# A delta-rule stage whose planner keeps a begun run of fill matmuls for three, with three more planning weights changed

## The chip, the cores and the metric

The kernel runs on one core of one Trainium2 chip. The metric is the device time of one execution in microseconds. Engines are called as in the profile: PE is TensorE (matmuls), PEld its weight loads, DVE is VectorE, ACT ScalarE, POOL GpSimd, and SP the engine that issues the DMAs. A line such as L886 is line 886 of the kernel before; from line 93 on, the same statement of the changed kernel stands 2 to 5 lines lower.

## What is computed

One layer of a diffusion backbone on 1024 latent tokens with a prefix of 256 context tokens, width 1024, 8 heads in each of two branches. Branch A is a gated delta rule, scanned forwards and backwards over chunks; branch B is differential softmax attention. Both are gated, projected, merged and projected once more. Cut to what matters here:

```python
h  = rms_norm(x)   * (1 + scale)   + shift      # 1024 latent tokens
hc = rms_norm(ctx) * (1 + scale_c) + shift_c    # 256 context tokens
qkv_a, z_a, a, b, q_b, k_b, v_b, z_b, gates = split_cols(h @ w_in)   # the context likewise

# branch A, for each direction and head, over chunks, one after the other
def step(s, xs_i):
    u_i, w_i, kd_i, gl_i, qd_i, qk_i = xs_i
    v_new  = u_i - w_i @ s
    s_next = s * exp(gl_i) + kd_i.T @ v_new
    return s_next, qd_i @ s + qk_i @ v_new

# branch B, for each head and block of queries
p = softmax(q @ k.T * scale)                    # two maps to a head
o = (p[0] - lam * p[1]) @ v

y_a = rms_norm(o_a) * silu(z_a);  y_b = rms_norm(o_b) * (1 - lambda_init) * silu(z_b)
merged = sigmoid(g_a) * (y_a @ w_oa) + sigmoid(g_b) * (y_b @ w_ob)
x = x + gate * (merged @ w_out)
```

## The kernel before

Everything is on one core, in float32 accuracy: a big matmul is made of three matmuls on a high and a low part of each operand (`wh`, `wl` of the weights, two tiles `hs` of the tokens). The program goes through five stages:

- **Front and first projections** (to about 420 us): tokens are normed and transposed, and the columns for branch A's q, k and v are projected, convolved and stored.
- **Delta-rule stage** (about 420 to 1300 us), the function `flow`, which the change edits. Here run side by side: the preparation of each head (`gdn_prep`: tiles `gram`, `pz`, `p2`, `p3`, `pu6` on PE), two scans, one for each direction (`scan`, L1292 on), the output of each chunk (`out_chunk`), the tails of finished heads (`tails`, tiles `oT`), and **fill**: projections that nothing in this stage needs soon. Fill is first attention's q, k and v columns (`part_flow`, 256-column matmuls) and then 32 units of gate columns (`fill_flow`, 512-column matmuls `mm<-hs,wh` and `mm<-hs,wl`; a unit is two times 24 of them).
- **Hand-over and attention** (about 1300 to 1770 us), planned by `turn_flow`: scores `s`, softmax, transposes `t`, values `v`, and as a filler the projection `ma` of branch A's output with `w_oa`.
- **End**: `mb` (branch B's projection) and `x`, `z` (the last one).

A step of a scan is a loop through three engines. PE makes `chain<-S,sk`; DVE makes `r` of it (L1314); PE makes `chain<-r,x`; ACT makes `vd` (L1323); PE makes `chain<-vd,kk`; DVE makes the next state `S` (L1336, for the first chunk of a head a copy, L1334). The first chunk of a head has no state and begins with `chain<-vv,x`, where `vv` comes by DMA from memory once the head before is through.

The weights of a fill unit come in two halves: a DMA into `hx`, a cast to `wh` on ACT (L885), and the rest `wl` on POOL for the first half and on DVE for the second (L886). There are two buffers, so the weights of unit i can be made when unit i-2 is done.

The order of all instructions is fixed when the program is built. Each activity is a stream of instructions with a planned duration; each stream has a bias in microseconds. `flow` takes, again and again, the stream whose next instruction could start first by the planner's own clocks, where the bias is added to the start: a negative bias lets a stream go first. Fill is the stream without a bias (`None`); to its start the constant `FB0` = 0.05 is added. The streams that make fill's weights have the bias `WB`. In attention `turn_flow` takes the engine that is free first and on it, of the instructions that can start, the one with the lowest bias; these biases are the table `ABIAS`, and each task's place in time is added to its bias. `outs` is the task that squares a finished pair of value blocks on ACT (tile `osq`, L1669), `gateq` the one that multiplies the same blocks by their gate on DVE (tile `oT`, L1676), and `sums` makes the sums of squares of it on PE (`v<-ct,osq`). The one bank of the values is free again when the gate and the sum have both read it.

On the chip each engine goes through its own list in order and waits, by semaphores, for what an instruction needs.

Of the kernel before, what the change touches and what calls it, by code (L numbers as in the profile page):

```python
# [34 lines left out]
PE, DVE, ACT, POOL, DMA, ADMA, DV2, PL1 = range(8)  # L35
# [8 lines left out]
class Block:  # L44
# [30 lines left out]
    def flow(self, until):  # L75


        clk = self.clk
        while not until():
            best = None  # L80
            for s in self.streams:
                self.ask(s)
            for s in self.streams:
                self.ask(s)
                h = s[2]
                if h is None or callable(h):
                    continue
                if s[3] is None:
                    s[3] = self.ready_at(h[0], h[2])
                start = self.begin_at(h[0], s[3])  # L90
                if s[1] is None:
                    start += self.FB0 if self.units_done < self.FT else self.FB1
                if h[0] == PE and len(h) > 4 and self.heat - self.HEAT * (start - clk[PE]) < 0:
                    start += self.COLD
                if best is None or start + (s[1] or 0.0) < best[0]:
                    best = (start + (s[1] or 0.0), s)
            assert best, "no stream can go on"
            self.step(best[1])

    def turn_flow(self, until):  # L100
# [613 lines left out]
    def run(self):  # L714
# [4 lines left out]
        with ExitStack() as left:  # L719
            self.hp, self.hs = self.spool(left, "hp"), {}  # L720
            self.hgroup(0)
            with ExitStack() as lw, ExitStack() as cx:
# [22 lines left out]
                with tc.manual_schedule(engines={E.PE, E.DVE, E.Activation, E.Pool, E.SP}):  # L745
# [25 lines left out]
                    def more():  # L771
                        yield lambda: sum(self.posted) == sum((NL if k == "q" else NT) // 2 for k, _ in parts)
                        cx.close()
                        self.gdn_more(gr)
                        yield lambda: False
                    for g, b in ((self.scan(0), "scan"), (self.scan(1), "scan"), (self.forever(self.outq[0]), "outq"),
# [4 lines left out]
                        self.stream(g, self.BIAS[b]) if g is not first else self.streams.append([g, self.BIAS[b], head, None])  # L781
                    self.stream(self.part_weights(parts), self.WB)
                    self.stream(self.weights(todo), self.WB)
                    self.stream(more())
                    self.stream(fill(), None)
                    self.MW = 2.5
                    self.flow(lambda: self.tailed == H and self.units_done >= len(todo) - self.LEFT)
                    gr.close()
# [647 lines left out]
    def named(self, n, gen):  # L1436
        s = self.entry[n] = [gen, self.ABIAS.get(n, 0), None, None]
        s[2] = next(gen, None)
        self.streams.append(s)

    def due(self, n, i):

        self.entry[n][1] = self.ABIAS.get(n, 0) + self.DUE * i

# [35 lines left out]
    SPI = 0.5  # L1480
    MW = 0.0
    LAND = 2.5
    WB = -0.17
    FT = 38
    LEFT = 3
    FB0 = 0.05
    FB1 = 0.36
    COLD = 0.4
# [246 lines left out]
    def side_start(self):  # L1735
# [10 lines left out]
    ONACT = (1, 2, 3)  # L1746
    TOL = 0.02
    PACE = 4.48
    ABIAS = dict(rels=-0.59, softs=8.84, norms=5.82, gateq=-27.29, sums=-18.71,
                 outs=-21.73, lows=-2.4, highs=-9.33, adds=36.19, scales=31.0, evs=22.29, mouts=-3.31,  # L1750
                 att_out=1.9, turns=3.19, scores=-21.22, merge=25.46)
    KEEP = 3

# [455 lines left out]
```

## Time and profile before

| what | value |
|---|---|
| median of 3 runs | 1941.17 us (1939.21 to 1942.13) |
| profiled execution, its own time | 1941.8 us |
| its span, first to last instruction | 1939.9 us |
| granted TensorE clock, mean | 0.999 |
| PE busy in the span | 1901.0 us, 98% |
| DVE, ACT, POOL busy | 75%, 55%, 35% |
| chain that ended last, PE's share | 83% |

PE is busy in almost the whole span, so the time is PE's work and the few places where PE waits. A matmul is shown from its start to a modelled end, and matmuls overlap; that is why the mean length of a 512-column matmul in the profile (390 ns) is longer than the distance from one to the next (about 0.23 us in an undisturbed run). A wait that is shorter than this overlap is not shown as idle. A 128-column float32 matmul goes through PE in two passes and is shown as two records.

### The profile page before, as it was taken

What the parts mean: (1) busy time and instruction counts of PE and PEld (TensorE: products, weight loads), DVE (VectorE), ACT (ScalarE), POOL (GpSimd) and SP (SyncE); (2) the same over time, 40 slices, a digit from 0 to 9 for tenths busy, and PEclk for the clock granted to TensorE, in tenths of its full rate; (3) what the DMA queues carried; (4) which work ended last, traced back from release to release, by engine and by line L of the source; (5) the groups of instructions that cost most, each with busy time, mean ns of one, the idle gap of its engine ahead of it and who ended that gap; (6) DMA issues with size and microseconds to landing.
All of it is one profiled execution on the core that took longest, in us unless ns stands there. A gap on an engine that the chain in (4) does not pass through costs nothing.

```text
span 1939.9 us, 37460 instructions
## 1 busy us (share of the span) xinstructions
PE 1901.0 (98%) x13807; PEld 1675.0 (86%) x13807; DVE 1453.6 (75%) x3613; ACT 1063.6 (55%) x2189; POOL 679.6 (35%) x610
## 2 busy tenths in 40 slices
PE   6999999999999999999999999999999999999999
PEld 4978888899999998888888888887997888888887
DVE  4687998957887888767864965337996979985577
ACT  4543444426233563677575655448885868883222
POOL 3200000005541342343433232326766657671203
PEclk9999999999999999999999999999999999999999
DMA  9144535574545557667686565665436474226542
GB/s 333 61 133 98 138 95 134 127 194 171 173 141 184 173 188 230 232 196 236 196 291 199 183 199 166 206 236 201 129 123 205 162 244 148 83 88 221 185 148 87
DMA packets 383038, 336.39 MB, mean 173 GB/s; under 512 B 142609, under 2 KB 323443, under 8 KB 381831
## 3 DMA queue, kind: packets, MB, share of 16 engines
q1 hardware_dynamic: 382855, 333.99, 54.9%
q8 instruction: 109, 1.79, 0.4%
q14 instruction: 74, 0.61, 0.1%
HBM read 222.14 MB, written 111.79 MB: 172 GB/s over the span
## 4 chain that ended last, share of the span: by engine, by line
PE 83%; DVE 6%; DMA 4%; ACT 3%; issue 2%; POOL 1%; SPq 1%; DVEq 0%; ACTq 0%; POOLq 0%
PE mm L56 42%; PE s L56 6%; PE v L56 5%; PE chain L56 5%; PE mb L56 5%; PE ma L56 4%; PE x L56 3%; PE t L63 3%; PE out L56 3%; PE gram L56 1%; DVE S L1565 1%; DVE ac L595 1%; PE tr L63 1%; PE pz L56 1%; PE mp L56 1%
## 5 line engine op out<-in xcount | busy, mean ns | idle before, releaser
L56 PE MATMUL mm<-hs,wh 128*128 128x512 f32 (+1 forms) x2048 | 648.2, 390 | 1.5 <-DVE hs L408 1.4
L56 PEld LDWEIGHTS mm<-hs,wh 128*128 128x128 f32 x2048 | 371.1, 189 | 58.7 <-DVE hs L408 2.0
L56 PE MATMUL mm<-hs,wl 128*128 128x512 f32 (+1 forms) x1024 | 397.3, 388 | 1.0 <-POOL wl L886 1.0
L56 PE MATMUL mm<-wh,hs 128*128 128x256 f32 (+1 forms) x1792 | 332.8, 286 | 0.2 <-ACT sq L978 0.2
L56 PEld LDWEIGHTS mm<-wh,hs 128*128 128x128 f32 x1792 | 280.8, 191 | 0.7 <-ACT sq L978 0.4
L1565 DVE TENSOR_SCALAR_CACHE_REDUCE S<-s,rsq 128x512 f32<-128x512 f32 (+1 forms) x384 | 239.6, 655 | 30.8 <-PE s L56 28.1
L56 PE MATMUL mm<-wl,hs 128*128 128x256 f32 (+1 forms) x896 | 255.7, 285 | 0.0
L1602 POOL TENSOR_TENSOR S<-S 128x1280 f32<-128x1280 f32 x64 | 189.0, 2956 | 92.2 <-ACT S L1595 91.0
L56 PEld LDWEIGHTS mm<-hs,wl 128*128 128x128 f32 x1024 | 193.7, 189 | 29.7 <-POOL wl L886 1.4
L1578 ACT ACTIVATE S<-S,mn 128x1280 f32<-128x1280 f32 x128 | 175.2, 1371 | 51.2 <-DVE mn L1577 50.7
L56 PEld LDWEIGHTS mm<-wl,hs 128*128 128x128 f32 x896 | 171.3, 191 | 0.1
L595 DVE SCALAR_TENSOR_TENSOR ac<-xc,convT,ac 128x1284 f32<-128x1284 f32 (+1 forms) x96 | 138.7, 1447 | 11.3 <-ACT ac L593 10.7
L56 PE MATMUL s<-kk,qh 128*128 128x512 f32 (+1 forms) x384 | 143.1, 373 | 1.6 <-DVE S L1565 1.4
L56 PE MATMUL s<-kk,ql 128*128 128x512 f32 (+1 forms) x384 | 133.5, 359 | 0.0
L1639 DVE TENSOR_TENSOR al<-t,ah 128x512 fp32r<-128x512 f32 (+1 forms) x192 | 106.8, 594 | 7.4 <-ACT ah L1634 6.1
L580 POOL MEMSET xc<- 128x2 f32 (+1 forms) x64 | 3.6, 100 | 299.8 <-ACT sq L629 113.6
L1160 DVE TENSOR_TENSOR ts<-ts,tmp 80x31 f32<-80x31 f32 (+15 forms) x248 | 94.0, 379 | 6.0
L1158 DVE TENSOR_TENSOR tmp<-ab,ts 80x31 f32<-80x31 f32 (+15 forms) x248 | 93.1, 375 | 6.8 <-DMA ab<-da 1.4
L1323 ACT ACTIVATE vd<-chain,edk 128x128 f32<-128x128 f32 x144 | 52.3, 371 | 78.0 <-PE chain L56 72.2
L56 PE MATMUL ma<-y,wh 128*128 128x512 f32 x256 | 93.1, 410 | 1.7 <-DVE g L1812 1.7
L1634 ACT CAST ah<-t 128x512 fp32r<-128x512 f32 (+1 forms) x192 | 88.1, 521 | 9.8 <-PE t L63 8.5
L56 PE MATMUL v<-al,vh 128*128 128x256 f32 x320 | 90.6, 283 | 0.7 <-DVE al L1639 0.7
(296 smaller groups left out, 4314.0 us busy)
## 6 DMA issues: line engine op xcount, KB each, us to landing
wr<-in_w_in_dram SPq DMA_DIRECT2D x48, 512.0 KB, 6.3
hx<-in_w_in_dram SPq DMA_DIRECT2D x64, 256.0 KB, 4.6
x<-xq SPq DMA_DIRECT2D x64, 256.0 KB, 5.0
X<-gcd SPq DMA_DIRECT2D x8, 1280.0 KB, 7.6
kd<-col SPq DMA_DIRECT2D x40, 256.0 KB, 2.2
xq<-X SPq DMA_DIRECT2D x16, 640.0 KB, 8.8
kk<-kd SPq DMA_DIRECT2D x16, 640.0 KB, 6.1
kq<-gkq SPq DMA_DIRECT2D x8, 1152.0 KB
```

The costliest lines, as they stand in the source:

```text
L56: self.nc.tensor.matmul(out, lhsT, rhs, start=start, stop=stop)
L63: self.nc.tensor.transpose(out, src, self.ident[:src.shape[0], :src.shape[0]])
L580: x["e"].append((yield PL1, 0.1, [old], lambda: nc.gpsimd.memset(xc[:, a:b], 0.0)))
L595: t = yield DV2, 1.21e-3 * wd, [t], lambda: nc.vector.scalar_tensor_tensor(ac[:, :wd], xc[:, j:j + wd], self.convw(j, x["ct"]), ac[:, :wd] ...
L1158: t = yield DV2, n * w / 960.0 + 0.08, [t if j else self.later(t, 2.5), t1], lambda: V.tensor_tensor(tv, ab[:, j + 1:, j:j + 1].to_broadca ...
L1160: t = yield DV2, n * w / 960.0 + 0.08, [t, t1], lambda: V.tensor_tensor(ts[:, j + 1:, :w], ts[:, j + 1:, :w], tv, ALU.subtract)
L1323: td = yield ACT, 0.251, [t], lambda: nc.scalar.activation(vd, pc[:, 1], AF.Copy, scale=self.edk[:, c, g:g + 1])
L1565: e = yield DVE, 0.675 if m == 512 else 0.408, [e, self.sfree[c].get(n - 4 + c)], lambda: self.nc.vector.tensor_scalar(x["S"][c][:, o:o + ...
L1578: x["x"].append((yield ACT, 1.36, [e], lambda: nc.scalar.activation(S, S, AF.Exp, bias=x["mn"][:, c:c + 1], scale=-1.0, accum_out=w["l0"][ ...
L1602: e = yield POOL, 2.9, [e], lambda: self.nc.gpsimd.tensor_tensor(S0, S0, S1, ALU.add)
L1634: e = yield ACT, 0.48 if nb == 4 else 0.27, [t, y["old", k]], lambda: self.nc.scalar.copy(y["ah", k][:, :, q], pv)
L1639: t = yield DVE, 0.603 if k < 2 else 0.322, [e, y["old", k]], lambda: self.nc.vector.tensor_tensor(y["al", k][:, :, q], pv, y["ah", k][:, ...
```

## The change

In `flow` the planner counts how many fill matmuls it has placed on PE one after the other (`streak`). While this count is 1 or 2, every other stream's PE instruction is put 0.5 us (`SWC`) later in the comparison; with 3 (`RUN`) it stands as before. The bias of the streams that make the weights goes from -0.17 to -0.06. In attention's table the bias of `gateq` goes from -27.29 to -16.59 and that of `outs` from -21.73 to -35.56. The work itself is the same.

```diff
                 if s[1] is None:
                     start += self.FB0 if self.units_done < self.FT else self.FB1
+                elif h[0] == PE and 0 < self.streak < self.RUN:
+                    start += self.SWC
                 if h[0] == PE and len(h) > 4 and self.heat - self.HEAT * (start - clk[PE]) < 0:
                     start += self.COLD
                 if best is None or start + (s[1] or 0.0) < best[0]:
                     best = (start + (s[1] or 0.0), s)
             assert best, "no stream can go on"
+            if best[1][2][0] == PE:
+                self.streak = self.streak + 1 if best[1][1] is None else 0
             self.step(best[1])
...
-    WB = -0.17
+    WB = -0.06
...
+    RUN, SWC, streak = 3, 0.5, 0
...
-    ABIAS = dict(rels=-0.59, softs=8.84, norms=5.82, gateq=-27.29, sums=-18.71,
-                 outs=-21.73, lows=-2.4, highs=-9.33, adds=36.19, scales=31.0, evs=22.29, mouts=-3.31,
+    ABIAS = dict(rels=-0.59, softs=8.84, norms=5.82, gateq=-16.59, sums=-18.71,
+                 outs=-35.56, lows=-2.4, highs=-9.33, adds=36.19, scales=31.0, evs=22.29, mouts=-3.31,
```

What this does to the order is shown at three places, all on PE. A row is an instruction with its line, output tile and input tiles; numbers tell buffers apart.

**First place: the end of the fifth unit's and the beginning of the sixth unit's gate columns, with both scans running.** Two chains, one for each direction, alternate with fill. Before:

```order
L56 MATMUL mm_9168<-hs_142,wh_7732 128x512
L56 MATMUL chain_9275<-S_9270,sk_9007 128x128
L56 MATMUL mm_9168<-hs_143,wh_7732 128x512
L56 MATMUL chain_9283<-S_9277,sk_9007 128x128
L56 MATMUL mm_9168<-hs_142,wl_7733 128x512
L56 MATMUL mm_9294<-hs_86,wh_7732 128x512
L56 MATMUL chain_9275<-r_9287,x_9130 128x128
L56 MATMUL chain_9283<-r_9292,x_9135 128x128
```

Of the change:

```order
L56 MATMUL mm_9138<-hs_143,wh_7719 128x512
L56 MATMUL mm_9138<-hs_142,wl_7720 128x512
L56 MATMUL chain_9231<-S_9222,sk_9017 128x128
L56 MATMUL chain_9237<-S_9226,sk_9017 128x128
L56 MATMUL chain_9231<-r_9247,x_8986 128x128
L56 MATMUL chain_9237<-r_9250,x_8990 128x128
L56 MATMUL out_9273<-S_9222,sq_9023 128x128
L56 MATMUL out_9278<-S_9226,sq_9023 128x128
L56 MATMUL chain_9231<-vd_9257,kk_9012 128x128
L56 MATMUL out_9273<-vn_9268,x_8986 128x128
L56 MATMUL chain_9237<-vd_9259,kk_9012 128x128
L56 MATMUL mm_9270<-hs_86,wh_7719 128x512
```

Before, single fill matmuls stand between the chains' rows, and the next unit (`mm_9294`) begins among them; now a full step of both chains stands without a fill matmul between two units.

**Second place: the same kind of boundary nine units later.** Before:

```order
L56 MATMUL chain_11706<-r_11721,x_11565 128x128
L56 MATMUL chain_11713<-r_11727,x_11584 128x128
L56 MATMUL mm_11625<-hs_143,wh_7732 128x512
L56 MATMUL mm_11625<-hs_142,wl_7733 128x512
L56 MATMUL mm_11750<-hs_86,wh_7732 128x512
L56 MATMUL mm_11750<-hs_87,wh_7732 128x512
```

Of the change:

```order
L56 MATMUL mm_11578<-hs_142,wl_7720 128x512
L56 MATMUL chain_11654<-r_11660,x_11436 128x128
L56 MATMUL chain_11666<-S_11662,sk_11412 128x128
L56 MATMUL chain_11666<-r_11675,x_11452 128x128
L56 MATMUL chain_11654<-vd_11673,kk_11410 128x128
L56 MATMUL chain_11666<-vd_11681,kk_11410 128x128
L56 MATMUL chain_11699<-S_11692,sk_11412 128x128
L56 MATMUL out_11700<-S_11648,sq_11414 128x128
L56 MATMUL out_11700<-vn_11684,x_11436 128x128
L56 MATMUL chain_11718<-S_11695,sk_11412 128x128
L56 MATMUL mm_11705<-hs_86,wh_7719 128x512
```

Before, fill went from one unit into the next without a break; now nine rows of the scans stand there, and in two of them a product follows directly on the one that it depends on by way of another engine.

**Third place: attention, the eighth pair of value blocks, from its last product to its sums of squares.** Before:

```order
L56 MATMUL v_16631<-ah_16618,vl_16053 128x256
L56 MATMUL s_16752<-kk_15673,qh_15672 128x512
L56 MATMUL s_16752<-kk_15673,ql_15710 128x512
L56 MATMUL s_16764<-kk_15673,qh_15672 128x256
L56 MATMUL s_16764<-kk_15673,ql_15710 128x256
L63 MATMUL t_16660<-ct_60,S_16456 128x128 x4
L63 MATMUL t_16777<-ct_60,S_16456 128x128 x4
L63 MATMUL t_16786<-ct_60,S_16456 128x128 x2
L56 MATMUL s_16796<-kk_15673,qh_15672 128x512
L56 MATMUL s_16796<-kk_15673,ql_15710 128x512
L56 MATMUL v_16631<-ct_60,osq_16757 128x1 x2
```

Of the change:

```order
L56 MATMUL v_16574<-ah_16563,vl_16065 128x256
L56 MATMUL ma_16470<-y_15459,wh_15973 128x512
L56 MATMUL ma_16470<-y_15459,wl_15974 128x512
L56 MATMUL v_16574<-ct_60,osq_16642 128x1 x2
L56 MATMUL ma_16669<-y_15347,wh_16440 128x512 x2
```

Before, sixteen matmuls stood between the last product and the sums; now two do, and the next group of `ma` begins right behind them.

## The prediction

> **What bounds the kernel now.** I read the engine shares first, then the same by stage, then the waits of PE in the stages that the change touches, then PE's order of time at its waits.
>
> ```profile
> PE 1901.0 (98%) x13807; PEld 1675.0 (86%) x13807; DVE 1453.6 (75%) x3613; ACT 1063.6 (55%) x2189; POOL 679.6 (35%) x610
> ```
>
> ```profile
> 745.00:1300.00 555.00, 551.67 (x4767) 480.23 (x4766) 352.45 (x1034) 329.99 (x962) 193.06 (x248) 1.00 0.68 213
> 1345.00:1790.00 445.00, 440.14 (x2815) 386.86 (x2814) 370.63 (x1211) 336.87 (x564) 279.13 (x143) 1.00 0.47 156
> ```
>
> The columns are the window, its length, busy time of PE, PEld, DVE, ACT and POOL, the granted clock, and DMA. The first row is the delta-rule stage with both scans: PE idles 555.00 - 551.67 = 3.3 us of it. The second is attention: 445.00 - 440.14 = 4.9 us. So PE's own work sets the time. The change leaves that work as it is; it can gain only where PE waits or changes from one kind of work to another, and lose only by new waits. Where PE waits in the scans and in attention:
>
> ```profile
> PE mm L56 <- POOL wl L886: 1.0, 1, 1.0
> PE chain L56 <- DMA sk<-gkq: 0.8, 1, 0.8
> PE chain L56 <- DMA vv<-gv: 0.7, 1, 0.7
> PE chain L56 <- DVE S L1334: 0.4, 1, 0.4
> PE chain L56 <- DVE r L1314: 0.2, 1, 0.2
> ```
>
> ```profile
> PE ma L56 <- DVE g L1812: 1.7, 2, 0.9
> PE s L56 <- DVE S L1565: 1.1, 4, 0.5
> ```
>
> Five waits in 555 us, and 2.8 us of those in attention: there is little to win, whatever moves.
>
> **Term 1, fewer runs of fill.** The price of a change between fill and chains comes from rows of a run of one and a run of two, and from a long run:
>
> ```profile
> 1289.85 8.62 PE mm L56 x38
> ```
>
> ```profile
> 1006.25 0.38 PE L56 MATMUL out<-S,sq 128*128 128x128 f32 x2
> 1006.39 0.48 PE L56 MATMUL mm<-hs,wh 128*128 128x512 f32 x1
> 1006.70 0.40 PE L56 MATMUL mm<-hs,wl 128*128 128x512 f32 x1
> 1006.94 0.38 PE L56 MATMUL chain<-vd,kk 128*128 128x128 f32 x2
> 1007.16 0.39 PE L56 MATMUL out<-vn,x 128*128 128x128 f32 x2
> ...
> 1008.28 0.39 PE L56 MATMUL chain<-S,sk 128*128 128x128 f32 x2
> 1008.42 0.48 PE L56 MATMUL mm<-hs,wh 128*128 128x512 f32 x1
> 1008.74 0.38 PE L56 MATMUL chain<-S,sk 128*128 128x128 f32 x2
> ```
>
> A fill matmul in a long run takes 8.62 / 38 = 0.227 us, a chain product 1007.16 - 1006.94 = 0.22. The run of two with the product ahead of it takes 1006.94 - 1006.25 = 0.69, against 0.22 + 2 x 0.227 = 0.674; the run of one takes 0.46 against 0.447. So a run costs some 0.015 us beside its work (0.01 to 0.02). Counted in the two orders, from the first `gram` row of PE to the last `oT` row, runs of 512-column fill between other work fall from 351 to 269: runs of one from 115 to none, of two from 92 to 1, of three up from 51 to 166. So the change does what it says. 82 x 0.015 = **-1.2 us** (bounds -0.8 and -1.6).
>
> The Trainium skill, "TensorE: Matmul & The Clock Gate" (Part 2: What happens when you issue a matmul), says that weight loads are pulled ahead of matmuls in flight and that back-to-back matmuls are spaced by their columns alone. By that rule this term would be nil and the sum 1.2 us higher; the trace does not quite agree, since the rows above show a small price, and I stay with them.
>
> **Term 2, chains with no fill between them.** A scan's loop has a length of its own, and where PE has less work between two of its rows, PE waits. The place where the kernel before has this shows the lengths:
>
> ```profile
> 1067.44 0.39 PE L56 MATMUL mm<-hs,wl 128*128 128x512 f32 x1
> 1067.67 0.38 PE L56 MATMUL chain<-vv,x 128*128 128x128 f32 x2
> 1067.89 0.39 PE L56 MATMUL chain<-vd,kk 128*128 128x128 f32 x2
> 1068.66 0.49 PE L56 MATMUL chain<-S,sk 128*128 128x128 f32 x2 [0.38 <-DVE S L1334]
> 1068.99 0.39 PE L56 MATMUL chain<-vd,kk 128*128 128x128 f32 x2
> 1069.13 0.48 PE L56 MATMUL mm<-hs,wh 128*128 128x512 f32 x1
> 1069.60 0.49 PE L56 MATMUL chain<-r,x 128*128 128x128 f32 x2
> ```
>
> From `chain<-vd` to `chain<-S` 1068.66 - 1067.89 = 0.77; from `chain<-S` to `chain<-r` 1069.60 - 1068.66 = 0.94; from the first product (`chain<-vv`, 1067.67) to its `chain<-vd` at 1068.99 1.32. This place loses 0.55 + 0.11 + 0.24 = 0.9 us against 0.22 for each product and 0.23 for the fill matmul.
>
> In the new order two places are tighter, the first two that the document shows. At the first, `chain_9231<-S` and its `<-r` have one other product between: 0.44 us of PE work for 0.94 needed, 0.5 lost; from there to `<-vd` stand four products, 0.88 for 1.32: 0.4. At the second, `chain_11666<-r` follows directly on its `<-S`: 0.94 - 0.22 = 0.7; its `<-vd` comes two products later: 1.32 - 0.44 = 0.9. Together 2.5. The place of the rows above keeps three fill matmuls in the new order, 0.9 of work for 1.32, and loses 0.4 in place of 0.9. Term 2: 2.5 + 0.4 - 0.9 = **+2.0 us** (bounds +0.5, if the 1.32 is only as long as it is because the product ahead of it waited, and +3).
>
> **Term 3, weights.** The longest wait of the scans is for weights:
>
> ```profile
> 1055.14 0.71 PE L56 MATMUL mm<-hs,wh 128*128 128x512 f32 x2
> 1056.85 0.50 PE L56 MATMUL mm<-hs,wl 128*128 128x512 f32 x1 [1.00 <-POOL wl L886]
> ```
>
> ```profile
> L885 ACT CAST wh<-hx x60: 600/618/642, 759.1 to 1296.8; 128x512 fp32r<-128x512 f32 x60
> L886 POOL TENSOR_TENSOR wl<-hx,wh x30: 1273/1290/1732, 759.8 to 1297.0; 128x512 fp32r<-128x512 f32 x30
> ```
>
> It costs 1056.85 - 1055.14 - 2 x 0.227 = 1.26, of which some 0.1 is the change of kinds ahead of it: 1.2. In the new order the casts of this unit stand behind an ACT row whose product is 12.8 us of PE work earlier (before 6.6). The weaker bias delays the weights at two other units, those of term 2: 2.5 and 2.2 us of PE work from that product to the unit's first matmul. Cast and rest take 0.62 + 1.29 = 1.9, and `wl` is read two matmuls (0.45) after the unit's start, which the waits of term 2 put off by 0.9 and 1.6 more. So no new wait follows, narrowly. **-1.2 us** (bounds -1.2, and +0.8 if both units wait for a us each).
>
> **Term 4, first chunks of a head.** Behind them `vv` must have landed:
>
> ```profile
> 921.01 0.48 PE L56 MATMUL mm<-hs,wh 128*128 128x512 f32 x1
> 922.20 0.68 PE L56 MATMUL chain<-vv,x 128*128 128x128 f32 x4 [0.71 <-DMA vv<-gv]
> ```
>
> This one loses 1.19 - 0.23 = 0.96. In the order, PE work from the head before to this row falls from 9.25 to 9.04 us, and at the head before that from 7.07 to 6.63; elsewhere it grows. **+0.4 us** (bounds -1 and +0.8).
>
> **Term 5, attention.** `outs` is sent first and `gateq` later. At the third place of the document two `ma` matmuls (0.45 us) stand between a pair's last product and its sums:
>
> ```profile
> 1472.32 0.28 PE L56 MATMUL v<-ah,vl 128*128 128x256 f32 x1
> 1472.64 0.39 ACT L1669 ACTIVATE osq<-v 128x256 f32<-128x256 f32 x1 [4.30 <-PE v L56]
> 1473.83 0.50 PE L56 MATMUL v<-ct,osq 128*128 128x1 f32 x4
> ...
> 1475.20 0.39 PE L56 MATMUL ma<-y,wl 128*128 128x512 f32 x1
> 1476.37 0.50 PE L56 MATMUL ma<-y,wh 128*128 128x512 f32 x1 [0.78 <-DVE g L1812]
> ```
>
> ACT begins 0.32 after the product's start and takes 0.39, and the sums come at most 1.5 after it; with 0.57 of work between them, PE waits between 0.2 and 0.9 there: 0.6. The lower rows show the single bank of `ma` asked for again at once: 1.17 from group to group where 0.23 is work. Such places are three in both orders. Banks of `s` asked for within 1.36 us of work are 10 before and 14 now, by sums of shortage 1 us more. Against it, the new `ma` wait stands behind the wait of the sums and is paid only once, -0.7. **+0.9 us** (bounds -2.5, if the new weights empty the 2.8 us of waits above, and +3).
>
> **Sum:** -1.2 + 2.0 - 1.2 + 0.4 + 0.9 = +0.9 us. The profiled execution took 1941.8 by its own time, so 1942.7; the median of the runs shown, 1941.17, is 0.6 lower. **Forecast 1942.0 us**, and with the terms' bounds taken together about 1938 to 1946: no change that can be told, since a measurement of this kernel tells some 0.2% (3.9 us) from none, that is under 1937.3 or over 1945.1.
>
> **Rivals.**
>
> *Faster: the waits go.* If the longer runs let scans and weights meet on time everywhere, the 3.3 us of idle in the scans and the 1.2 of runs go, and with a third of attention's 4.9: 1941.2 - 6.1 = 1935. For it: fewer changes of kind, and the one long weight wait has no counterpart. Against it: the two places without fill.
>
> *Slower: the gate comes late in attention.* The values' bank comes free when DVE has multiplied by the gate, and DVE, busy 370.63 of 445.00, now takes that task later. If each of the 32 pairs hands the bank over 0.2 us too late for PE, 6.4 us are lost: 1941.2 + 6.4 = 1948. It decides where less PE work stands between a pair's sums and the next pair's products than the gate and the sum need. Against it: this work is 3.47 us at the least in both orders.
>
> *Slower: the clock drops at a place without fill.* The hand-over shows what that costs:
>
> ```profile
> PE t L63 <- ACT zo L1039: 1.9, 1, 1.9
> ```
>
> ```profile
> 1323.60:1327.00 3.40, 3.40 (x14) 3.11 (x13) 0.42 (x1) 2.55 (x5) 1.92 (x1) 0.50 0.71 242
> ```
>
> After a wait of 1.9 us PE ran 3.4 us at half clock, 1.7 us lost. Two such windows at the places of term 2 give 1942.0 + 3.4 = 1945.4. Against it: the waits of 1.0 and 0.7 us in the scans left the clock at 1.00 in the stage's row, and the new ones are in pieces of under 1 us. The Trainium skill, same page (Part 1: The HAM clock gate), states windows of about 3.4 us after which an inactive PE is put to half rate; the row agrees in length and rate, though the wait ahead of it was shorter than a window. By that rule the places of term 2 would not drop the clock.
>
> **How the numbers follow.** No change that can be told 0.46, the waits go 0.27, the gate late 0.18, the clock 0.09. So faster by over 0.2% is 0.27, within 0.2% 0.46, slower 0.27. The range must leave out no more than 2 in 10; it reaches into both sides, 1936 to 1947.5.
>
> **What would show it.** Right: PE's busy time in the scans about as before; waits of `chain` for `r` and `vd` at two new places around 825 and 1008 us, in all 2 to 3 us; no wait for `wl` over 1 us; PE's idle time in attention between 4 and 7 us; the clock at half only in the hand-over. Wrong: waits for `wl` at those two units (term 3), a long wait of `v` for `oT` in many pairs (the gate), a clock under 1.00 in the scans, or attention's idle time well under 4 us.

## The result, and the profile after

The changed kernel takes 1964.01 us (median of 4 runs, 1962.98 to 1968.14); beside it the kernel before took 1940.99 (4 runs). The ratio is 1.0122 [1.0108, 1.0135]: 23 us slower, where 1942.0 was forecast. The profiled execution took 1962.98 by its own time, with a span of 1961.2 and a granted clock of 0.997.

The page's first part, and then the table by stage: window, its length, busy time of PE, PEld, DVE, ACT and POOL, granted clock, DMA share, GB/s.

```profile
PE 1912.4 (98%) x13807; PEld 1679.3 (86%) x13807; DVE 1450.7 (74%) x3613; ACT 1060.7 (54%) x2187; POOL 676.2 (34%) x610
```

```profile
450.00:750.00 300.00, 293.58 (x2881) 288.16 (x2880) 244.97 (x606) 127.57 (x292) 109.83 (x84) 1.00 0.53 165
750.00:1300.00 550.00, 543.45 (x4714) 474.39 (x4713) 351.85 (x1039) 323.78 (x954) 187.59 (x246) 0.99 0.66 207
...
1350.00:1790.00 440.00, 431.91 (x2754) 374.77 (x2752) 365.69 (x1210) 335.60 (x567) 280.63 (x141) 1.00 0.45 151
```

The counts are those of before but for two activation table loads fewer on ACT (29 in place of 31), and PE's share is still 98%: the shares hide a loss of 21 us. PE idles 6.4 and 6.6 us in the first two stretches and 8.1 in attention (before: 2.5, 3.3 and 4.9). A matmul that is late shows partly as a longer one, so from here on another measure is used, called **lost time**: for each PE record the distance to the start of the next, less what its kind takes undisturbed in the kernel before (0.227 us for 512 columns, 0.119 for 256, 0.111 for one pass of a 128-column product, 0.109 for a transpose, smaller kinds by their mean there). By it PE's work is 1859.8 us in every run. The rest of the span is lost; the table leaves out only the time ahead of the first PE record and behind the start of the last one, some 9.5 us. By stretch, in us:

| kernel | median | to 450 | 450 to 750, heads prepared | 750 to 1300, scans | 1300 to 1350, hand-over | 1350 to first `mb`, attention | end |
|---|---|---|---|---|---|---|---|
| before | 1941.0 | 19.0 | 7.3 | 16.2 | 8.4 | 17.2 | 2.6 |
| changed | 1964.0 | 17.4 | 11.6 | 24.0 | 6.7 | 29.4 | 2.6 |
| run_alone | 1960.2 | 18.6 | 8.1 | 21.7 | 18.1 | 17.3 | 2.6 |
| bias_alone | 1960.1 | 18.7 | 12.0 | 18.9 | 9.5 | 26.1 | 2.6 |
| att_of_before | 1952.0 | 18.6 | 11.6 | 25.1 | 6.4 | 18.4 | 2.6 |
| att_of_changed | 1949.8 | 18.6 | 8.4 | 15.5 | 7.3 | 26.8 | 2.6 |
| act_first | 1960.1 | 18.2 | 12.1 | 20.9 | 7.9 | 26.5 | 2.6 |
| weights_first | 1960.3 | 18.2 | 8.6 | 17.6 | 15.3 | 27.3 | 2.6 |
| weights_middle | 1949.3 | 18.4 | 8.9 | 20.0 | 10.3 | 17.8 | 2.6 |
| run_of_four | 1966.9 | 18.3 | 8.3 | 21.6 | 25.6 | 21.2 | 2.6 |
| ma_paced | 1977.3 | 19.9 | 12.7 | 22.4 | 6.3 | 42.8 | 2.6 |
| before_paced | 1962.6 | 18.3 | 7.0 | 14.4 | 8.7 | 37.9 | 2.6 |
| ma_of_before | 1996.3 | 18.9 | 12.1 | 24.2 | 7.5 | 60.9 | 2.6 |
| ma_of_changed | 1995.6 | 18.7 | 13.0 | 23.6 | 6.9 | 60.1 | 2.6 |

The spread of the measure can be read from it: five of these kernels have the changed kernel's order up to the hand-over and lose 22.4 to 25.1 us in the scans, three have that of before and lose 14.4 to 16.2. The changed kernel's 21.3 us more of span are thus about +7.8 in the scans, +4.3 where heads are prepared, +12.2 in attention, and -3.3 in the front and the hand-over.

PE's longest waits in the first two stretches and the hand-over, engine and line waited for, us in total, times, longest:

```profile
PE chain L56 <- ACT vn L1331: 4.8, 2, 3.1
PE t L63 <- ACT zo L1043: 2.4, 1, 2.4
PE tr L63 <- DVE X L1134: 1.7, 1, 1.7
PE tr L63 <- DVE Z L1221: 1.7, 1, 1.7
PE tr L63 <- POOL fin L1012: 1.6, 2, 1.4
```

The first row is the two places of term 2, and it is not the loop's own length that makes it. The order of time at the first place, PE and ACT:

```profile
828.31 0.75 PE L56 MATMUL chain<-r,x 128*128 128x128 f32 x4 [0.22 <-DVE r L1318]
...
828.47 0.61 ACT L889 CAST wh<-hx 128x512 fp32r<-128x512 f32 x1
...
829.10 1.28 ACT L1113 ACT_TABLE_LOAD   x1
...
830.39 1.27 ACT L1113 ACTIVATE X<-X 128x1280 f32<-128x1280 f32 x1
...
831.57 0.60 ACT L889 CAST wh<-hx 128x512 fp32r<-128x512 f32 x1
832.08 0.36 ACT L1327 ACTIVATE vd<-chain,edk 128x128 f32<-128x128 f32 x1
...
832.64 0.80 PE L56 MATMUL chain<-vd,kk 128*128 128x128 f32 x2 [3.14 <-ACT vn L1331]
```

From `chain<-r` to `chain<-vd` it takes 832.64 - 828.31 = 4.33 us, where the prediction took 1.32 from a place with nothing ahead of `vd` on ACT. Here the next unit's casts, a load of the activation table and the exponential of the next head stand ahead of it. At the second place it is the same with another load (before `zo`):

```profile
1014.65 0.38 PE L56 MATMUL chain<-r,x 128*128 128x128 f32 x2
...
1014.88 0.39 PE L56 MATMUL chain<-S,sk 128*128 128x128 f32 x2
1015.00 1.28 ACT L1043 ACT_TABLE_LOAD   x1
...
1016.30 0.60 ACT L1043 ACTIVATE zo<-mm 128x512 f32<-128x512 f32 x1
1016.79 0.61 ACT L889 CAST wh<-hx 128x512 fp32r<-128x512 f32 x1
...
1017.30 0.37 ACT L1327 ACTIVATE vd<-chain,edk 128x128 f32<-128x128 f32 x1
...
1017.88 0.91 PE L56 MATMUL chain<-vd,kk 128*128 128x128 f32 x4 [1.68 <-ACT vn L1331]
```

At each of the two PE's clock fell to half, as it did once more in attention:

```profile
831.50:838.40 6.90, 5.75 (x20) 5.11 (x21) 3.33 (x8) 5.57 (x19) 1.23 (x2) 0.51 0.80 196
1019.20:1022.70 3.50, 3.38 (x13) 3.00 (x13) 3.04 (x9) 3.01 (x11) 0.00 (x0) 0.51 0.54 138
1418.70:1422.10 3.40, 3.40 (x14) 2.80 (x13) 2.40 (x7) 3.40 (x7) 1.57 (x2) 0.52 1.02 346
```

That is 6.8 + 3.4 + 3.4 = 13.6 us at half clock. The first 1.1 us of it lie in the wait itself (831.5 to 832.64), so some 6.3 us are lost by it, against 1.7 before. The stretch 825 to 840 loses 6.7 us and 1010 to 1023 5.1 (before 0.7 and 0.4).

### The profile page after: what moved, and what is told of

It reads as the page before. It is cut to its first block, busy times and chain, and to the rows that moved or that the text cites. A ratio compares the mean times of both kernels' runs of the same rounds, so it can differ in the third digit from the quotient of the medians.

```text
span 1961.2 us, 37474 instructions
## 1 busy us (share of the span) xinstructions
PE 1912.4 (98%) x13807; PEld 1679.3 (86%) x13807; DVE 1450.7 (74%) x3613; ACT 1060.7 (54%) x2187; POOL 676.2 (34%) x610
## 4 chain that ended last, share of the span: by engine, by line
PE 78%; DVE 10%; issue 4%; ACT 4%; DMA 3%; POOL 1%; SPq 1%; ACTq 0%; DVEq 0%; POOLq 0%
PE mm L56 41%; PE chain L56 5%; PE s L56 5%; PE mb L56 5%; PE v L56 5%; PE x L56 3%; PE ma L56 3%; PE out L56 3%; PE t L63 3%; DVE S L1570 2%; PE gram L56 1%; DVE al L1644 1%; DVE ac L599 1%; PE pz L56 1%; PE tr L63 1%
## 5 line engine op out<-in xcount | busy, mean ns | idle before, releaser
L56 PE MATMUL mm<-hs,wh 128*128 128x512 f32 (+1 forms) x2048 | 639.7, 388 | 1.5 <-DVE hs L412 1.4
L1340 DVE SCALAR_TENSOR_TENSOR S<-S,egl,chain 128x128 f32<-128x128 f32 x128 | 42.6, 345 | 70.3 <-PE chain L56 67.8
```

The costliest lines, as they stand in the source:

```text
L56: self.nc.tensor.matmul(out, lhsT, rhs, start=start, stop=stop)
L1340: t = yield DVE, 0.263, [t], lambda: V.scalar_tensor_tensor(Sn, S, self.egl[:, c, g:g + 1], pc[:, 2], ALU.mult, ALU.add)
```

## The experiments

**The parts of the change by themselves.** `run_alone` is the changed kernel with the old bias and the old table, `bias_alone` the kernel before with the new bias.

```diff
 run_alone                        bias_alone
-    WB = -0.06                   -    WB = -0.17
+    WB = -0.17                   +    WB = -0.06
```

> The changed kernel with the weights' bias back at -0.17 and attention's two weights back; of the change only the rule of three is left. Scan stage is counted from the first gram to the last fill matmul: 873 us before, 886 changed; attention from there to the first mb: 449 before, 459 changed. Theory A (the rule of three uses up a unit's matmuls and leaves the chains bare, and ACT's queue then makes the wait long): its order has two bare steps of its own (near 820 and 1140 us), so the scan stage stays 3 to 12 us over 873. Theory B (the weaker bias makes the weights late): scan stage back at 873 within 2. No forecast for attention; its order is a third one.

> The kernel before with the weights' bias at -0.06 alone (attention's two weights are as before; undone or not, they change no row of any engine's order). Theory A: no bare step stands in its order beyond those of before, so the scan stage is 873 within 3 and the clock stays full in it. Theory B: the scan stage is 880 or more, with waits behind weight casts. Attention's order has its ma matmuls distributed as in the changed kernel: if that order is the slow one, attention takes about 459 here too.

Measured: `run_alone` 1960.16 us (ratio 1.009 [1.0071, 1.0109]), `bias_alone` 1960.06 (1.0094 [1.0075, 1.0114]). Each part alone costs nearly all of it, but in other places. From the first `gram` to the last fill matmul `run_alone` took 870.4 us, less than either theory allowed, and `bias_alone` 881.9, theory B's number, though no wait for a weight cast is listed. By the table, what is lost where heads are prepared goes with the bias (12.0 and 11.6 with -0.06, 7.3 and 8.1 with -0.17), and most of what is lost in the scans with the rule (21.7 and 24.0 against 16.2 and 18.9). But the waits of the scans are not the same ones: with the rule alone the longest is for a transfer (`x<-xq`, 2.6 us), and those for `vn` come to 0.6 us; the two long waits for `vn` came only with both parts. The rest is in the later stages: `bias_alone` has an attention like the changed kernel's (26.1), `run_alone` one that costs no more than before (17.3) but a hand-over that loses 18.1. There PE waits for an input:

```profile
PE s L56 <- DMA ql<-qd: 8.9, 1, 8.9
```

The DMAs of `ql` stand on SP behind two of `gt<-zo`, issued over 17 us, and behind the stores `ya` (start, length, engine, line):

```profile
1290.07 17.25 SPq L1045 DMA_DIRECT2D gt<-zo  x2
...
1319.81 0.32 SPq L1414 DMA_DIRECT2D ya<-oa  x1
1320.22 1.25 SPq L1516 DMA_DIRECT2D ql<-qd  x2
```

In the kernel before the first `ql` was issued at 1289.41, ahead of the long issues of `gt`.

The third part, attention's table, does nothing at all. `turn_flow` looks at a bias only among instructions of one engine that can start within 0.02 us of the first one (`TOL`), and with `gateq` and `outs` put back the changed kernel has the same order on all five engines; the kernel before with the new two keeps its own. Attention's order is nevertheless another one, so it comes from the other two edits, by the clocks with which the planner arrives there.

**Attention's order by itself.** The sequence of the planner's choices in attention and the end was written down for both kernels and laid down in the other, so that up to the hand-over the order is that of one, and from there that of the other.

```diff
+            if self.turns_ is not None:
+                s = self.streams[ord(TURNS[self.turns_]...) - 48]
+                self.turns_ += 1
+                self.step(s)
+                continue
             self.step(min(...))
```

> The changed kernel up to the hand-over, then the order of attention and the end word for word as in the kernel before. Theory C (attention is slower by the order it got): attention 449 within 3, the whole about 1954. Theory D (attention is slower by what the delta stage hands over, late transfers or a busy engine): attention stays at 457 or more, the whole 1962 or more.

> The kernel before up to the hand-over, then the order of attention and the end word for word as in the changed kernel. Theory C: attention 458 within 3, the whole about 1951. Theory D: attention 449 to 451, the whole 1941 to 1943.

Measured: `att_of_before` 1951.96 us (1.0052 [1.0032, 1.0071]), `att_of_changed` 1949.77 (1.0044 [1.0028, 1.0061]). The order of attention costs 1964.0 - 1952.0 = 12 us one way and 1949.8 - 1941.0 = 9 the other; the stretches ahead of it change the rest. From the last fill matmul to the first `mb` it took 447.7 and 457.3 us, as theory C has it. So it is a cost of the order, and about half of the slowdown. Of the 12 us, 1.7 is the half-clock window at 1418.6, which `att_of_changed` does not have.

**What in that order costs.** The filler `ma` differs most: after every eighth score block the kernel before has placed 0, 32, 63, 157, 192, 267, 295, 312 of its matmuls, the changed one 9, 45, 133, 168, 255, 288, 312, 312, none in the last eight. In the last 100 us before `mb` PE has 72 `ma` matmuls in place of 96, 5.4 us less work, and loses 10.4 us in place of 6.0, with DVE as busy as before (84.1 and 83.5 us). Two kernels pace `ma`:

```diff
-            yield lambda: len(self.groups) > self.KEEP or self.scored == H * NL
+            yield lambda: len(self.groups) > self.KEEP and self.scored >= 5.0 * (16 - len(self.groups)) or self.scored == H * NL
```

> The changed kernel, in which a group of `ma` (24 matmuls) may not begin before five score blocks for each group taken before it are done. By the order, `ma` matmuls placed after every eighth block become 9, 45, 115, 144, 189, 224, 259, 307 in place of 9, 45, 133, 168, 255, 288, 312, 312. Theory C, attention is slower because the filler `ma` is used in bursts and is gone by block 50: the last 75 us before `mb` lose 5 us less than their 10.2, the burst around 1560 us costs under 2 in place of 4.3, and the time is 1954 to 1958. Rival, the loss is in how scores, softmax and values meet, whatever fills: attention stays within 2 us of its 458.8 and the time at 1962 to 1966.

> The kernel before with the same pace for `ma`: 0, 32, 63, 157, 189, 224, 259, 307 after every eighth block in place of 0, 32, 63, 157, 192, 267, 295, 312. Theory C: the filler lasts to the last blocks, whose idle time of 4.4 us falls by 1 to 3: 1938 to 1941 against 1941.0. Rival, the filler held back is missed in the middle: 1942 to 1946.

Measured: 1977.26 us (1.0183 [1.0167, 1.0198]) and 1962.62 (1.0106 [1.009, 1.0123]). Both missed the theory and the rival: with filler kept back, attention loses 42.8 and 37.9 us. Two more kernels mix the orders: `ma` with its weights and inputs placed as in one kernel, all else of attention as in the other, on the changed kernel's scans.

> The changed kernel with a hybrid order in attention: scores, softmax, transposes, values and gates as the changed kernel has them among themselves, and `ma` with its weights, inputs and outputs placed among them where the kernel before has it (0, 32, 63, 157, 192, 267, 295, 312 matmuls after every eighth block in place of 9, 45, 133, 168, 255, 288, 312, 312). Up to the hand-over all is as in the changed kernel. Theory C, the place of `ma` decides: attention falls from 458.8 to 448 to 451 us and the time to 1952 to 1956 (with all of attention in the order of before it was 1952.0). Rival, the order of scores, softmax and values among themselves decides: attention stays at 457 or more, the time at 1962 to 1966. Rival, only the two together fit: it is slower than 1966.

> The reverse: up to the hand-over the changed kernel; in attention scores, softmax, transposes, values and gates in the order of before, and `ma` with its weights, inputs and outputs where the changed kernel has it. Theory C: attention at 456 us or more, the time at 1960 to 1965. Rival, the order of the others decides: attention at 448 to 451, the time at 1952 to 1955.

Measured: 1996.26 us (1.0275 [1.0257, 1.0293]) and 1995.56 (1.0269 [1.025, 1.0288]), attention losing 60.9 and 60.1. For the first the third case holds, that only the two together fit; the second had no such case, and missed both of its ranges. The mixing was not exact: on the chip `ma` stood, after every eighth block, at 0, 24, 63, 157, 192, 267, 295, 312 and at 9, 48, 120, 168, 264, 288, 312, 312. And no run tells what the mixing costs by itself, since both hybrids lose some 31 us more in attention than the dearer of the whole orders. So attention's loss isn't shown to lie in `ma` or in the others singly, and what makes one whole order some 10 us dearer than the other stays open.

**The places without fill: ACT's queue.** In `act_first` the order of ACT alone is changed, at the two places (rows of ACT, first place):

```diff
 CAST wh<-hx 128x512
+ACTIVATE vd<-chain,edk 128x128
+COPY vn<-chain 128x128
+ACTIVATE vd<-chain,edk 128x128
+COPY vn<-chain 128x128
+CAST wh<-hx 128x512
 ACT_TABLE_LOAD
 ACTIVATE X<-X 128x1280
-CAST wh<-hx 128x512
-ACTIVATE vd<-chain,edk 128x128
-COPY vn<-chain 128x128
-ACTIVATE vd<-chain,edk 128x128
-COPY vn<-chain 128x128
```

> The changed kernel with another order on ACT alone, at the two places of term 2: there `vd` and `vn` of both chains and the second cast of the next unit stand ahead of the table load and exponential (first place) or of the table load and `zo` (second place), and eight of the `X` rows behind the next step's `vd`. All other engines keep their rows. Theory A, the places cost what they do because `vd` stood behind 3.8 us (4.3 from product to product) and 3.8 us of other work on ACT: the wait of `chain` for `vn` falls from 4.8 to under 1.5 us, at least two of the three half-clock windows (6.83 and 3.41 us) go, and the time falls by 6 to 8 us from 1964.0, to about 1957. Rival, two steps without fill are slow by their own loop through three engines: the waits stay at 4 us or more in other rows, the time at 1962.5 to 1965.5. Rival, ACT is full there and the delay goes on to the next step: half of it comes back, 1960 to 1962.

Measured: 1960.06 us (1.0098 [1.0081, 1.0115]), 4 less than the changed kernel; the scans lose 20.9 us in place of 24.0. Its waits of PE in the scans (its line numbers are larger, by the list of choices in its head), then the first place as a row by stretch, of `act_first` and of the changed kernel:

```profile
PE chain L189 <- DVE r L1472: 2.4, 4, 1.1
PE out L189 <- DVE oa L1514: 1.7, 2, 1.3
...
PE chain L189 <- ACT vn L1485: 0.4, 1, 0.4
```

```profile
825.00:840.00 15.00, 13.06 (x85) 11.03 (x84) 8.12 (x24) 14.22 (x41) 5.80 (x6) 1.00 0.86 271
```

```profile
825.00:840.00 15.00, 11.64 (x60) 10.17 (x59) 6.64 (x20) 13.22 (x38) 5.17 (x6) 0.77 0.79 240
```

The second place, again of `act_first` and of the changed kernel:

```profile
1010.00:1023.00 13.00, 10.34 (x122) 8.49 (x122) 6.26 (x18) 12.56 (x33) 2.69 (x3) 1.00 0.60 172
```

```profile
1010.00:1023.00 13.00, 10.73 (x59) 9.08 (x58) 5.88 (x16) 11.86 (x31) 2.74 (x3) 0.87 0.69 205
```

The wait for `vn` fell from 4.8 to 0.4 us, all three half-clock windows went (one of 3.4 us came in the hand-over), and at the first place PE began 85 records in place of 60 in the same 15 us. The cause of the wait for `vn` is thus shown: the work ahead of it on ACT. But ACT is busy 14.22 of 15.00 us at the first place and 12.56 of 13.00 at the second: at the first its table load and exponential now delay `oa`, and DVE's `r` stands behind `oa`. In the scans the waits for `r` and `oa` are 2.4 + 1.7 us, where the changed kernel has 0.7 for `r`. Between the theory (6 to 8 us) and the second rival (half comes back, 1960 to 1962) the second rival has the number.

By lost time less than half comes back at the two places: 825 to 845 falls from 6.9 to 4.4 us and 1010 to 1027 from 5.3 to 4.6 (before 0.7 and 0.5). Four more kernels with the changed kernel's rows there lose 5.6 to 7.1 and 4.7 to 5.4, so at the second place the gain can't be told from the spread. Another order on ACT thus moves the wait, and most of the loss stays while ACT is busy almost throughout; whether less work for ACT there would end it was not tested.

**The places without fill: enough fill.** Three kernels keep the rule and give the weights more precedence, so that by the order fewer steps stand without fill.

```diff
 weights_first        weights_middle       run_of_four
-    WB = -0.06       -    WB = -0.06      -    WB = -0.06
+    WB = -0.5        +    WB = -0.3       +    WB = -0.8
                                           -    RUN, SWC, streak = 3, 0.5, 0
                                           +    RUN, SWC, streak = 4, 0.5, 0
```

> The changed kernel with the bias of the weights at -0.5 in place of -0.06, so that they go ahead of more. By the order the scans have 286 runs of fill and steps that fall short of the loop's lengths (0.94 and 1.32 us) by 1.1 us in all; the changed kernel has 269 and 4.5, before 351 and 1.0. Attention has the changed kernel's distribution of `ma`. Theory: what the rule costs in the scans comes from steps without fill where weights are late, so the stretch from 750 to 1300 us loses no more than before's (16.2 us beyond PE's work, the changed kernel 23.8), the three half-clock windows go, and with attention's 10 us and at most the 4 us that the weaker bias costs ahead of the scans the time is 1949 to 1955. Rival, the rule itself costs the scans: 1957 or more.

> The changed kernel with the bias of the weights at -0.3. By the order the scans have 268 runs of fill (changed kernel 269, before 351) and 2.3 us of shortage (4.5 and 1.0), spread over five steps around one place, none below 0.67 us for 1.32 needed. Attention comes out close to before's: 95 in 100 of PE's rows between the first `ma` and the first `mb` stand in the same sequence (changed kernel 49 in 100), and `ma` after every eighth block is 2, 32, 63, 157, 192, 267, 295, 312. Theory, the 10 us of attention belong to its order, which follows from the state in which the planner comes to it, and not to the rule: attention at 447 to 451 us, the stretch from 750 to 1300 at 14 to 18 us beyond PE's work (before 16.2, changed kernel 23.8), and the time at 1938 to 1944; if `ql` comes late in the hand-over, as with the rule alone and with the bias at -0.5, 1946 to 1952. Rival, the rule slows attention whatever its order: 1950 or more with attention at 456 or more and no wait for `ql`.

> A run of four in place of three, and the bias of the weights at -0.8. By the order 247 runs of fill in the scans and 0.04 us of shortage, and `ma` spread evenly in attention (14, 48, 96, 144, 192, 240, 288, 312, as with the rule alone). Theory: without steps that fall short the longer runs give what term 1 says, 104 x 0.015 = 1.6 us, and no wait of over 0.5 us stands in the scans; attention loses no more than before. If the hand-over has its inputs in time: 1936 to 1941, the one version that may beat both. If SP's queue brings `ql` late, as with the rule alone (8.9 us of wait and 10 us of half clock): 1946 to 1951.

Measured: `weights_first` 1960.25 us (1.0094 [1.0078, 1.0111]), `weights_middle` 1949.29 (1.0046 [1.0029, 1.0063]), `run_of_four` 1966.92 (1.0128 [1.0112, 1.0143]). All three times missed their ranges; the stretches say why.

`weights_first`: the scans lose 17.6 us (changed kernel 24.0, before 16.2) with the clock at 1.00 throughout, as the theory has it, to within 1.4. Its time lies where the rival had it (1957 or more), but not for the rival's reason, since it is lost elsewhere: in the hand-over, where `ql` is late again by 6.4 us (the theory had left that out), and in an attention of the changed kernel's kind (27.3).

`weights_middle`: attention, whose order is nearly that of before, loses 17.8, so the rule does not slow attention by itself. No wait for `ql` stands in the hand-over, so 1938 to 1944 was its range. The scans lose 20.0, over the expected 18, and again by `vd` behind a table load, an exponential and two casts:

```profile
1007.29 1.28 ACT L1113 ACT_TABLE_LOAD   x1
...
1007.83 0.28 PE L56 MATMUL chain<-r,x 128*128 128x128 f32 x1
...
1008.59 1.27 ACT L1113 ACTIVATE X<-X 128x1280 f32<-128x1280 f32 x1
...
1009.76 1.12 ACT L889 CAST wh<-hx 128x512 fp32r<-128x512 f32 x2
...
1010.79 0.36 ACT L1327 ACTIVATE vd<-chain,edk 128x128 f32<-128x128 f32 x1
...
1011.35 0.49 PE L56 MATMUL chain<-vd,kk 128*128 128x128 f32 x2 [1.83 <-ACT vn L1331]
```

From `chain<-r` to `chain<-vd` 1011.35 - 1007.83 = 3.5 us: the same mechanism at a third place, in another order.

`run_of_four`: outside the stretch 1150 to 1175 the scans lose 14.8 us (before 16.0), as expected of them; but in that stretch they lose 6.8 (before 0.2), with one wait for nothing that the profile shows and 6.8 us of half clock from 0.6 us before its end:

```profile
PE p L56 <- issue: 3.5, 1, 3.5
```

The hand-over loses 25.6: `ql` late by 9.3 us, a wait of 9.5 of `oT` for `oa`, and the clock at half for 23.9 us. No version beat the kernel before.

## Why the prediction was wrong

**What bounds the kernel.** Right that PE's work sets the time, and that little idle time could be won. But the conclusion from it, that small sums of waits decide, left the risk of long ones out.

**Term 1, fewer runs.** The runs fell as counted. Its -1.2 us can't be told by itself: outside the two places the scans lost 24.0 - 6.7 - 5.1 = 12.2 us against 16.2 - 0.7 - 0.4 = 15.1, so 2.9 less, where terms 1, 3 and 4 with the third place of term 2 made -1.2 - 1.2 + 0.4 - 0.5 = -2.5. The sum agrees, but that isn't shown to be more than luck: kernels with one and the same order there differ by up to 2.7 us in the scans (22.4 to 25.1).

**Term 2, chains with no fill.** The first step that failed. The places were the right ones (the waits stand at 829 to 833 and at 1016 to 1018 us), and the size was not: 2.5 us for the two, measured (6.7 + 5.1) - (0.7 + 0.4) = 10.7. The lengths of the loop were taken from a place where ACT was free, and the step asked only what PE has between two rows. What stands ahead of `vd` on ACT was not looked up, though the order gives it: 3.8 us at the first place (cast 0.61, table load 1.28, exponential 1.27, cast 0.60), 2.5 at the second (table load 1.28, `zo` 0.60, cast 0.61). `act_first` shows that this makes the wait for `vn`, and also that with `vd` and `vn` put ahead most of the loss stays, as waits for `r` and `oa`, with ACT busy almost throughout. So what the step had wrong is ACT: it counted PE's work alone and took ACT as free. The half clock made some 4.5 of the 10.7 us: half of the 9.1 us that it lasted at the two places while PE had work.

**Term 3, weights.** Right: no wait for `wl` stands in the scans. But only the gate units' weights were costed. The same `WB` is the bias of the weights of the earlier fill, attention's q, k and v columns, which runs where heads are prepared, and there some 4 us were lost (waits of `tr` for `X`, `Z` and `fin`, 5.0 us in the rows above; in the kernel before 1.1, for `fin`): the second step that failed, an effect of the edit that no term had. `bias_alone` against `run_alone` shows that it goes with `WB` (12.0 and 8.1 us); how later weights bring these waits about was not traced.

**Term 5, attention.** The third step that failed, and the largest: +0.9, measured +12. It gave two biases as the reason of a moved order, and they move nothing; the order moved by the other two edits, through the state in which the planner came to it. That the order costs 9 to 12 us is shown, what in it does is not. The few places that were costed from rows (sums of squares, banks of `s`) don't stand for an order in which half of the rows changed their sequence.

**The rivals.** None was the result. "The clock drops at a place without fill" did happen, at both of its places and with more than its price (two windows of 3.4 us): 6.8 and 3.4. Its objection, that the waits are in pieces of under 1 us, rested on term 2. "The gate comes late" rested on an edit without effect. "The waits go" may have in the scans beside the two places (2.9 us, about the spread of the measure).

**The range** took the bounds of each term, and none of these was open to a wait that another engine's queue makes: term 2's upper bound was +3.

## What to carry to other kernels

Where a change takes the cover from a loop through several engines, its length is not the sum of its latencies: on each engine of the loop, look in the new order at what stands ahead of the loop's instruction, here table loads and long activations, and at how full that engine is around the place, and add the half clock that came with waits of that size. Look up every reader of a changed constant, and test whether an edited weight moves any row before giving it a cost. Where a planner chooses greedily by its own clocks, one edit can give every later stage another order; here that was worth 9 to 12 us in attention, far more than the edit was for, so such a change should be judged by stages, with the later ones' order held fixed.

## What the runs showed of the hardware that was not expected

The clock fell to half with waits shorter than 3.4 us, the least for which it then stayed so: for 6.8 us with a wait of 3.1 (it fell 2.0 us into the wait), for 3.4 behind one of 1.7, and for 3.4 at 1418.6 us, where the list of waits between 1405 and 1425 has 0.7 and 0.4. It did not fall behind the wait of 1.8 at 1011 us in `weights_middle`. The same rows do not always give the same: of the five kernels with the changed kernel's order the first place had 6.8 us of half clock in two and 3.4 in three. And with the order of before the clock fell at 600.5 us in `att_of_changed` and not in the kernel before; there PE's wait that nothing in the profile explains was 1.9 us in the one and 0.9 in the other. The Trainium skill, "TensorE: Matmul & The Clock Gate" (Part 1: The HAM clock gate), states that half rate follows at least one idle window of about 3.4 us and that the window runs freely; the length agrees, the idle window doesn't.

A load of the activation table took 1.28 us each time, and the activation behind it began 0.01 us after its end (829.10 + 1.28 = 830.38; 830.39). The Trainium skill, "ScalarE: Activation LUTs" (What ACT_TABLE_LOAD costs), gives 1.28 us for the load, which the rows agree with, and 1.38 for a drain beside it, which they don't show.
